# A relu-and-row-sum kernel whose first 8 MB block is loaded through two DMA queues instead of one

## The chip, the core and the metric

The kernel runs on one core of one Trainium2 chip. The core has five engines with their own instruction streams: TensorE (PE), VectorE (DVE), ScalarE (ACT), GpSimd (POOL) and SyncE (SP), and 16 DMA engines that move data between the chip's main memory (HBM) and the core's working memory (SBUF, 128 partitions). A DMA is issued by an instruction on one of the engines and goes into that engine's queue; when its data have landed it raises a semaphore on which other instructions wait. The metric is the device time of one execution in microseconds (us); lower is better. Before the change it is 161.0 us, the median of three runs (161.0, 161.0 and 161.11).

## The reference

```python
batch, seq, dim = 32, 512, 1024
x = randn(batch, seq, dim)          # float32, 64 MiB
relu_x = np.maximum(x, 0)
return np.sum(relu_x, axis=-1)      # (32, 512), float32
```

Each of the 16384 rows of 1024 numbers is clamped at zero from below and added up. The kernel reads 67.1 MB and writes 64 KB; there is nothing else to compute.

## The kernel before

**Tiling.** The 16384 rows are cut so that every partition of SBUF gets 128 rows: 16 rows from the first 2048 (`xf`), and 112 from the other 14336 (`xv`). In both parts the rows of one partition lie one behind the other in HBM. Seven blocks of 16 rows per partition (`ROWS = 16`, 8 MB each, 64 KB in one piece for each partition) are followed by a tail of 8 rows (4 MB), 4 rows (2 MB), and a last stretch of 4 rows, which comes in four loads that get ever smaller (1151, 436.5, 259 and 201.5 KB). Three buffers (`io0` to `io2`, `NBUF = 3`) of 8 MB take the blocks in turn.

**Who does what.** In blocks 0 and 1 ScalarE clamps the whole block in place with one instruction (`clamp`, line 145), and VectorE then adds up its 16 rows with one reduction (`total`, line 153). In blocks 2 to 4 the same is done in two halves of 8 rows, in block 5 in two pieces of 7 rows with two more rows left to ScalarE alone, which clamps and sums a row with one instruction (`act_row`, line 160). In block 6 and the tail ScalarE and VectorE each take whole rows (`act_row` and `dve_row`, line 168). The last stretch is divided among ScalarE, VectorE and GpSimd. TensorE does a few matmuls near the end whose results are not used.

**What sets the order.** All loads are issued by SyncE (`load`, line 104), so they stand in one queue in program order. The loads of blocks 0, 1 and 2 have a buffer each and wait for nothing. The load of block 3 waits on VectorE's semaphore until VectorE has finished block 0, whose buffer it overwrites; blocks 4, 5, 6 and the first tail load wait in the same way for blocks 1, 2, 3 and 4. Each load has a semaphore of its own (`sems.loads[n]`), which the DMA raises by 16 when it is complete.

**How it starts.** `open_without_barrier` takes the barriers of the program's opening out and moves SyncE's first load (`EARLY = 1`) in front of SyncE's first instruction, so the load of block 0 is the first thing that SyncE does. ScalarE's first instruction of this kernel's work is the load of its function table (`preload_act_table`, line 143). It waits for the semaphore of block 0's load (16), and stands for the wait of the first clamp too. The partial sums are collected in `res` and stored by three DMAs, two after the tail loads have been issued and one at the very end (line 116).

Of the kernel before, what the change touches and what calls it, by code (L numbers as in the profile page):

```python
# [5 lines left out]
RELU = mybir.ActivationFunctionType.Relu  # L6
# [3 lines left out]
ROWS = 16  # L10
NBUF = 3
# [14 lines left out]
MIDDLE_ACT, END_ACT = 214, 321  # L26

EARLY = 1
N_MM, MM_COLS = 8, 512


def kernel(tc: tile.TileContext, x: bass.AP, out: bass.AP):
    nc = tc.nc
    sems = Semaphores(tc)

    tc.close()
    tc.compile()
    nc.cur_bb = nc.bb_map[tc.start_bb_name]
    body = nc.cur_bb.bb.instructions
    ends = list(body)  # L40
    body.clear()
    n_stores = relu_sum(nc, sems, x, out)
    body.extend(ends)


    nc.cur_bb = nc.bb_map[tc.start_bb_name + "_end"]
    nc.cur_bb.bb.instructions.clear()
    nums = sorted(s.num for s in (*sems.loads, sems.act, sems.dve))
    cleared = range(nums[0], nums[-1] + 1)
    assert len(cleared) == len(nums)  # L50
    nc.sync.sem_clear(cleared)
    nc.sync.wait_ge(sems.stored, 16 * n_stores).then_inc(sems.stored, -16 * n_stores)
    open_without_barrier(tc, EARLY)

# [11 lines left out]
def relu_sum(nc, sems: Semaphores, x: bass.AP, out: bass.AP):  # L66
# [23 lines left out]
    def rows(m, n):  # L90
        if m < ROWS:
            return xf[:, m : m + n, :]
        return xv[:, m - ROWS : m - ROWS + n, :]

    def sums(m, n):
        if m < ROWS:
            return of[:, m : m + n], res[:, m : m + n]
        return ov[:, m - ROWS : m - ROWS + n], res[:, m : m + n]

    n_load = n_act = n_dve = n_store = 0  # L100

    def load(dst, src, after=None):
        nonlocal n_load
        dma = nc.sync.dma_start(out=dst, in_=src)  # L104
        if after:
            dma.wait_op(sems.dve, after[1], "sem-ge")
        dma.then_inc(sems.loads[n_load], 16)
        n_load += 1
        return sems.loads[n_load - 1]

    def store(m, n, act, sem, count):
        nonlocal n_store
        dst, src = sums(m, n)
        if act:
            nc.sync.wait_ge(sems.act, act)
        nc.sync.dma_start(out=dst, in_=src).wait_op(sem, count, "sem-ge").then_inc(
            sems.stored, 16
        )
        n_store += 1
# [20 lines left out]
    def clamp(ap, loaded):  # L140
        nonlocal n_act
        if n_act == 0:
            nc.scalar.preload_act_table(RELU).wait_op(loaded, 16, "sem-ge")  # L143
            loaded = None
        i = nc.scalar.activation(out=ap, in_=ap, func=RELU)  # L145
        if loaded is not None:
            i.wait_op(loaded, 16, "sem-ge")
        i.then_inc(sems.act, 1)
        n_act += 1

    def total(ap, m, n):
        nonlocal n_dve
        nc.vector.tensor_reduce(  # L153
            out=res[:, m : m + n], in_=ap, axis=mybir.AxisListType.X, op=ADD
        ).wait_op(sems.act, n_act, "sem-ge").then_inc(sems.dve, 1)
        n_dve += 1

    def act_row(ap, accum_out, loaded):
        nonlocal n_act
        i = nc.scalar.activation(out=ap, in_=ap, func=RELU, accum_out=accum_out)  # L160
        if loaded is not None:
            i.wait_op(loaded, 16, "sem-ge")
        i.then_inc(sems.act, 1)
        n_act += 1

    def dve_row(ap, accum_out, loaded):
        nonlocal n_dve
        i = nc.vector.tensor_scalar(  # L168
            out=ap,
            in0=ap,  # L170
            scalar1=0.0,
            scalar2=None,
            op0=MAX,
            op1=ADD,
            accum_out=accum_out,
        )
        if loaded is not None:
            i.wait_op(loaded, 16, "sem-ge")
        i.then_inc(sems.dve, 1)
        n_dve += 1  # L180
# [11 lines left out]
    freed = []  # L192
    m = 0
    for j in range(NB):
        buf = bufs[j % NBUF]
        loaded = load(buf[:, :, :], rows(m, ROWS), j >= NBUF and freed[j - NBUF])
        c = 0
        act_waits = dve_waits = loaded
        for n in TWO[j]:
            clamp(buf[:, c : c + n, :], act_waits)  # L200
            total(buf[:, c : c + n, :], m + c, n)
            act_waits = None
            c += n
        for _ in range(ACT[j]):
            act_row(buf[:, c, :], res[:, m + c : m + c + 1], act_waits)
            act_waits = None
            c += 1
        for _ in range(DVE[j]):
            dve_row(buf[:, c, :], res[:, m + c : m + c + 1], dve_waits)
            dve_waits = None  # L210
            c += 1
        assert c == ROWS
        freed.append((n_act, n_dve))
        m += ROWS
# [3 lines left out]
    buf = bufs[NB % NBUF]  # L218
    c = 0
    for n in TAIL:  # L220
        loaded = load(
            buf[:, c : c + n, :], rows(m, n), None if c else freed[NB - NBUF]
        )
# [9 lines left out]
    src = rows(m, 4).rearrange("p c d -> p (c d)")  # L233
    at = c * D
# [5 lines left out]
    loaded = load(flat[:, at : at + head], src[:, :head])  # L240
# [6 lines left out]
        out=clamped, in0=clamped, scalar1=0.0, scalar2=None, op0=MAX  # L247
    ).wait_op(loaded, 16, "sem-ge").then_inc(sems.end, 1)
    for lo, hi, n, first, second in (
# [3 lines left out]
        loaded = load(flat[:, at + lo : at + hi], src[:, lo:hi])  # L253
        act_part(flat[:, at + lo : at + lo + n], last[:, first : first + 1], (loaded, 16))
        dve_part(flat[:, at + lo + n : at + hi], last[:, second : second + 1], (loaded, 16))
    loaded = load(last[:, 2 : 2 + n_last], src[:, middle:end])
    assert loaded is sems.end

    store(0, ROWS, freed[0][0], sems.dve, freed[0][1])
    store(ROWS, NT - ROWS - 2, sums_act, sems.dve, sums_dve)


    all_there = (sems.end, 16 + 6)
    nc.vector.scalar_tensor_tensor(  # L266
        out=clamped,
# [6 lines left out]
    ).wait_op(*all_there, "sem-ge").then_inc(sems.end, 1)  # L274
    act_part(last[:, 2 + LAST_DVE :], res[:, NT - 1 : NT], all_there)
    store(NT - 2, 2, 0, sems.end, 16 + 6 + 2)
    return n_store


def open_without_barrier(tc: tile.TileContext, n_loads: int):  # L280

    SP = mybir.EngineType.SP
    blocks = tc.nc.main_func.blocks
    opening = blocks[0].instructions
    body = next(b for b in blocks if b.name == tc.start_bb_name).instructions
    for i in list(opening):
        if isinstance(i, (mybir.InstDrain, mybir.InstEventSemaphore)):
            opening.remove(i)  # L290
    loads = [i for i in body if i.engine == SP][:n_loads]
    for i in loads:
        assert isinstance(i, mybir.InstDMACopy)
        body.remove(i)
    at = next(n for n, i in enumerate(opening) if i.engine == SP)
    opening[at:at] = loads


# [28 lines left out]
```

## Time and profile before

| | |
|---|---|
| time, median of 3 runs | 161.0 us (161.0 to 161.11) |
| span of the profiled execution (first to last instruction) | 159.9 us |
| time of the runs that lies outside such a span | 161.0 - 159.9 = 1.1 us |
| time that the DMA queue's packets took, as a share of 16 engines' span | 97.8% |
| VectorE busy | 118.7 us (74%) |
| ScalarE busy | 103.6 us (65%) |
| HBM read | 67.11 MB, 420 GB/s over the span |

The page gives one execution, with the span from the first instruction to the last; the profiled execution has no other time of its own on the page. Busy shares are averages over the whole span. "Idle before" is the time in which an engine stood still ahead of a group of instructions, with what ended it. In the view by windows, the span is cut at given times; each row has the busy time of each engine with the number of its instructions in brackets, the granted TensorE clock, the share of the 16 DMA engines and GB/s. A DMA packet is booked in that view, with all its bytes and all its time, in the window in which it begins. In a short window the share can so be far over 1, and the GB/s say how many packets began there: a packet of block 0 is one partition's 64 KB (65,536 bytes).

### The profile page before, as it was taken

How to read it: one execution, taken by the hardware profiler on the slowest of the kernel's cores; microseconds unless marked ns; L12 is line 12 of the kernel's file. 1: busy time of each engine (PE TensorE's matmuls, PEld its weight loads, DVE VectorE, ACT ScalarE, POOL GpSimd, SP SyncE). 2: the span in 40 equal slices, each digit the busy share in tenths (PEclk: the TensorE clock that was granted, in tenths of full speed). 3: DMA queues.
4: the chain of work that ended last, by engine and by line, in shares of the span. 5: the costliest groups of instructions: out<-in, count | busy, mean ns of one | idle time of the engine just before them, and what ended most of it. 6: DMA issues, size and time to landing. Idle time of an engine off the chain costs nothing.

```text
span 159.9 us, 157 instructions
## 1 busy us (share of the span) xinstructions
PE 8.6 (5%) x16; PEld 3.6 (2%) x16; DVE 118.7 (74%) x44; ACT 103.6 (65%) x53; POOL 1.0 (1%) x5
## 2 busy tenths in 40 slices
PE   0000000000000000000000000000000000000695
PEld 0000000000000000000000000000000000000241
DVE  0000000006999799999999999999999799999986
ACT  0000049993599807997099950999429993397995
POOL 0000000000000000000000000000000000000001
DMA  8996996996996997999979979969969969899993
GB/s 279 508 492 295 524 492 295 524 492 295 525 492 295 524 475 311 524 393 393 525 328 459 508 344 459 508 295 508 492 295 524 492 295 524 377 402 402 428 396 110
DMA packets 2304, 67.18 MB, mean 420 GB/s; under 512 B 640, under 2 KB 768, under 8 KB 1024
## 3 DMA queue, kind: packets, MB, share of 16 engines
q1 hardware_dynamic: 2304, 67.18, 97.8%
HBM read 67.11 MB, written 0.07 MB: 420 GB/s over the span
## 4 chain that ended last, share of the span: by engine, by line
DMA 45%; DVE 45%; ACT 9%; SPq 1%; issue 0%
DMA io<-in_x_dram 45%; DVE res L153 43%; ACT io L145 9%; DVE io L168 1%; SPq L104 1%; DVE io L127 1%; DVE io L266 0%
## 5 line engine op out<-in xcount | busy, mean ns | idle before, releaser
L153 DVE TENSOR_REDUCE res<-io 128x8 f32<-128x8192 f32 (+2 forms) x10 | 101.1, 10173 | 39.2 <-ACT io L145 39.2
L145 ACT ACTIVATE io<-io 128x8192 f32<-128x8192 f32 (+2 forms) x10 | 81.8, 8218 | 25.9 <-DMA io<-in_x_dram 25.9
L160 ACT ACTIVATE io<-io 128x1024 f32<-128x1024 f32 x18 | 18.8, 1042 | 6.6 <-DMA io<-in_x_dram 6.6
L186 PE MATMUL ps<-io 128*128 128x512 f32 x16 | 8.6, 698 | 149.5 <-DVE io L168 149.5
L168 DVE TENSOR_SCALAR_CACHE_REDUCE io<-io 128x1024 f32<-128x1024 f32 x14 | 16.2, 1215 | 0.5 <-DMA io<-in_x_dram 0.4
L143 ACT ACT_TABLE_LOAD x1 | 1.3, 1283 | 22.3 <-DMA io<-in_x_dram 22.3
L186 PEld LDWEIGHTS ps<-io 128*128 128x128 f32 x16 | 3.6, 231 | 153.7 <-DVE io L168 149.5
L160 ACT ACTIVATION_READ_ACCUMULATOR io<-io 128x1 f32 x18 | 3.3, 186 | 0.0
L246 POOL TENSOR_SCALAR io<-io 128x254 f32<-128x254 f32 x1 | 0.8, 841 | 155.4 <-DMA io<-in_x_dram 155.4
L168 DVE DVE_READ_ACCUMULATOR io<-io 128x1 f32 x14 | 1.2, 82 | 0.0
L127 DVE TENSOR_SCALAR_CACHE_REDUCE io<-io 128x552 f32<-128x552 f32 (+1 forms) x2 | 1.1, 594 | 0.0
L122 ACT ACTIVATE io<-io 128x321 f32<-128x321 f32 (+1 forms) x2 | 0.9, 426 | 0.1
L266 DVE SCALAR_TENSOR_TENSOR io<-last,io 128x254 f32<-128x254 f32 x1 | 0.4, 423 | 0.0
L122 ACT ACTIVATION_READ_ACCUMULATOR io<-io 128x1 f32 x2 | 0.4, 186 | 0.0
L122 ACT ACTIVATE last<-last 128x153 f32<-128x153 f32 x1 | 0.3, 330 | 0.0
L122 ACT ACTIVATION_READ_ACCUMULATOR last<-last 128x1 f32 x1 | 0.2, 187 | 0.0
L127 DVE DVE_READ_ACCUMULATOR io<-io 128x1 f32 x2 | 0.2, 82 | 0.0
L311 POOL MEMSET const-uint8-127<- 128x1 uint8 x1 | 0.1, 102 | 0.0
L311 POOL MEMSET const-bfloat16-1.0<- 128x1 bf16 x1 | 0.1, 101 | 0.0
L311 POOL MEMSET const-float32-0.0<- 128x1 f32 x1 | 0.1, 99 | 0.2 <-issue 0.2
L311 POOL MEMSET const-float32-1.0<- 128x1 f32 x1 | 0.1, 98 | 0.0
L266 DVE DVE_READ_ACCUMULATOR io<-last,io 128x1 f32 x1 | 0.1, 82 | 0.0
## 6 DMA issues: line engine op xcount, KB each, us to landing
io<-in_x_dram SPq DMA_DIRECT2D x1, 4096.0 KB, 23.7
io<-in_x_dram SPq DMA_DIRECT2D x1, 2048.0 KB, 28.3
io<-in_x_dram SPq DMA_DIRECT2D x1, 1151.0 KB, 30.6
io<-in_x_dram SPq DMA_DIRECT2D x1, 436.5 KB, 31.2
io<-in_x_dram SPq DMA_DIRECT2D x1, 259.0 KB, 31.4
last<-in_x_dram SPq DMA_DIRECT2D x1, 201.5 KB, 31.4
io<-in_x_dram SPq DMA_DIRECT2D x7, 29.0
out_dram<-res SPq DMA_DIRECT2D x1, 55.0 KB, 1.6
```

Source lines behind the costliest of these rows:

```text
L104: dma = nc.sync.dma_start(out=dst, in_=src)
L122: nc.scalar.activation(out=ap, in_=ap, func=RELU, accum_out=accum_out).wait_op(*after, "sem-ge").then_inc(sems.end, 1)
L127: i = nc.vector.tensor_scalar(out=ap, in0=ap, scalar1=0.0, scalar2=None, op0=MAX, op1=ADD, accum_out=accum_out,)
L143: nc.scalar.preload_act_table(RELU).wait_op(loaded, 16, "sem-ge")
L145: i = nc.scalar.activation(out=ap, in_=ap, func=RELU)
L153: nc.vector.tensor_reduce(out=res[:, m : m + n], in_=ap, axis=mybir.AxisListType.X, op=ADD).wait_op(sems.act, n_act, "sem-ge").then_inc(se ...
L160: i = nc.scalar.activation(out=ap, in_=ap, func=RELU, accum_out=accum_out)
L168: i = nc.vector.tensor_scalar(out=ap, in0=ap, scalar1=0.0, scalar2=None, op0=MAX, op1=ADD, accum_out=accum_out,)
L186: i = nc.tensor.matmul(ps[:, :], rows_of[:, 0, :P], rows_of[:, 1, :MM_COLS], start=True, stop=True)
L246: nc.gpsimd.tensor_scalar(out=clamped, in0=clamped, scalar1=0.0, scalar2=None, op0=MAX).wait_op(loaded, 16, "sem-ge").then_inc(sems.end, 1)
L266: nc.vector.scalar_tensor_tensor(out=clamped, in0=last[:, : 2 + LAST_DVE], scalar=0.0, in1=clamped, op0=MAX, op1=ADD, accum_out=res[:, NT ...
L311: nc = _bacc.Bacc("TRN2", target_bir_lowering=False, num_devices=1)
```

## The change

The load of block 0 is split in two by partitions. The even partitions (64 of them, 4 MB) are loaded by a DMA from SyncE's queue, the odd ones (64, 4 MB) by a DMA from ScalarE's. Both raise the same semaphore by 16, and the first wait on it (the function table's on ScalarE) is for 32 instead of 16. `open_without_barrier` now moves the first load of SyncE and the first of ScalarE in front of the first instruction of their engines. All other loads, the stores and the computation are as they were.

```diff
 EARLY = 1
+QUEUES = 2
...
+    def load_spread(dst, src):
+        nonlocal n_load
+        for q, engine in enumerate((nc.sync, nc.scalar)):
+            engine.dma_start(out=dst[q::QUEUES], in_=src[q::QUEUES]).then_inc(
+                sems.loads[n_load], 16
+            )
+        n_load += 1
+        return sems.loads[n_load - 1]
...
     def clamp(ap, loaded):
         nonlocal n_act
         if n_act == 0:
-            nc.scalar.preload_act_table(RELU).wait_op(loaded, 16, "sem-ge")
+            nc.scalar.preload_act_table(RELU).wait_op(loaded, 16 * QUEUES, "sem-ge")
             loaded = None
...
     for j in range(NB):
         buf = bufs[j % NBUF]
-        loaded = load(buf[:, :, :], rows(m, ROWS), j >= NBUF and freed[j - NBUF])
+        first = j == 0
+        if first:
+            loaded = load_spread(buf[:, :, :], rows(m, ROWS))
+        else:
+            loaded = load(buf[:, :, :], rows(m, ROWS), j >= NBUF and freed[j - NBUF])
...
-    SP = mybir.EngineType.SP
...
-    loads = [i for i in body if i.engine == SP][:n_loads]
-    for i in loads:
-        assert isinstance(i, mybir.InstDMACopy)
-        body.remove(i)
-    at = next(n for n, i in enumerate(opening) if i.engine == SP)
-    opening[at:at] = loads
+    for engine in (mybir.EngineType.SP, mybir.EngineType.Activation):
+        loads = [i for i in body if i.engine == engine][:n_loads]
+        for i in loads:
+            assert isinstance(i, mybir.InstDMACopy)
+            body.remove(i)
+        at = next(n for n, i in enumerate(opening) if i.engine == engine)
+        opening[at:at] = loads
```

## The prediction

> **What bounds the kernel now.** I read the page's DMA line and queue share first:
>
> ```profile
> DMA  8996996996996997999979979969969969899993
> q1 hardware_dynamic: 2304, 67.18, 97.8%
> ```
>
> The 16 DMA engines are occupied for 97.8% of the span; the dips are an effect of booking a packet where it begins. Next the timeline between 37 and 125 us:
>
> ```profile
> 37.45 17.22 DVE L153 TENSOR_REDUCE res<-io 128x16 f32<-128x16384 f32 x1 [37.45 <-ACT io L145]
> 41.60 13.86 ACT L145 ACTIVATE io<-io 128x16384 f32<-128x16384 f32 x1 [4.18 <-DMA io<-in_x_dram]
> 54.70 70.41 SPq L104 DMA_DIRECT2D io<-in_x_dram  x6
> 60.95 13.95 ACT L145 ACTIVATE io<-io 128x8192 f32<-128x8192 f32 x2 [5.49 <-DMA io<-in_x_dram]
> 80.29 13.95 ACT L145 ACTIVATE io<-io 128x8192 f32<-128x8192 f32 x2 [5.39 <-DMA io<-in_x_dram]
> 99.65 13.95 ACT L145 ACTIVATE io<-io 128x8192 f32<-128x8192 f32 x2 [5.41 <-DMA io<-in_x_dram]
> ```
>
> The clamps start when a block lands, and blocks land every 19.35 us (60.95 - 41.60, 80.29 - 60.95). An 8 MB block is 128 packets of 64 KB, 8 for each of the 16 engines, so a packet takes 19.35 / 8 = 2.42 us, which is 27.1 GB/s per engine and 434 GB/s in all. ScalarE waits some 5.4 us for each block: compute is not the bound. The load of block 3 is issued at 54.70, while the block before it lands at 60.95, so the queue holds over 6 us of work. The chain of waits names VectorE for 43%, but only as the one that freed a buffer in time; the tail load that it released at 124.29 took 23.7 us to land by the table of DMA issues, though its own 8 packets per engine of half the size need 8 x 1.21 = 9.7 us: it stood in a queue that had not run dry. The end is thus: start of the DMA engines + 64 packets' worth of bytes on the slowest of them + the last arithmetic.
>
> Last the start, in windows:
>
> ```profile
> 0.00:1.00 1.00, 0.00 (x0) 0.00 (x0) 0.00 (x0) 0.00 (x0) 0.19 (x4) 1.00 0.00 0
> 1.00:1.50 0.50, 0.00 (x0) 0.00 (x0) 0.00 (x0) 0.00 (x0) 0.00 (x0) 1.00 4.62 1573
> 1.50:2.00 0.50, 0.00 (x0) 0.00 (x0) 0.00 (x0) 0.00 (x0) 0.00 (x0) 1.00 1.52 524
> 3.90:4.20 0.30, 0.00 (x0) 0.00 (x0) 0.00 (x0) 0.00 (x0) 0.00 (x0) 1.00 2.02 874
> 4.20:4.60 0.40, 0.00 (x0) 0.00 (x0) 0.00 (x0) 0.00 (x0) 0.00 (x0) 1.00 3.78 1638
> 4.60:4.80 0.20, 0.00 (x0) 0.00 (x0) 0.00 (x0) 0.00 (x0) 0.00 (x0) 1.00 0.00 0
> 4.80:5.00 0.20, 0.00 (x0) 0.00 (x0) 0.00 (x0) 0.00 (x0) 0.00 (x0) 1.00 1.51 655
> ```
>
> GB/s times window over 65,536 bytes gives the packets that begin: 12 between 1.0 and 1.5 us, 4 between 1.5 and 2.0. A first packet takes 4.62 x 0.5 x 16 / 12 = 3.08 us, 0.66 more than a later one. Second packets begin on 14 engines between 3.9 and 4.6, and on the last two between 4.8 and 5.0. These two stay behind for good, since all do the same work at the same pace, and a load is complete only with them.
>
> **The change part by part.** The sum is made against the profiled 159.9 us, and 161.0 - 159.9 = 1.1 us outside the span is carried over to compare with the median.
>
> *One more DMA on ScalarE.* SyncE's load issues take 0.33 to 0.49 us (0.41 median). ScalarE's next work, the table load, waits until 22.27 us, so the issue costs nothing there; uncovered it would be 0.5 us.
>
> *When the odd half starts.* No row shows when ScalarE begins; GpSimd's first row is at 0.23 us, so I take some 0.2 us after SyncE. An engine has an even packet to move until 3.9 us at the earliest, so an odd packet that is ready by 2 us or so costs nothing. The bounds are -0.4 (ScalarE's half lets engines begin one issue earlier) and +0.7; I take 0.
>
> *SyncE's queue.* The loads of blocks 1 and 2 stand behind a DMA of half the size and are issued no later. The wait for 32 ends with the later half. If the DMA engines take the two queues' packets in turn, the eight packets of block 0 on each engine still go first, and block 0 lands where it did.
>
> *How 64 rows fall to 16 engines.* This decides. The whole load gives each engine 8 of 128 partitions; each half gives it 4 of 64, and the trace doesn't say which. In all stages the pace is 2.42 us per packet on every engine, but with the whole load an engine and its group of partitions are one to one, so the rows can't tell an engine's limit from a limit of the way into a group of 8 partitions. If the limit is the engine's, or the halves are dealt to the same groups, the cost is 0. If the limit is the group's, and the 64 rows are dealt in another pattern, two engines write into one group at a time while another group gets nothing. Each then has half of the 27.1 GB/s, and the 8 packets of block 0 take 8 x 4.84 instead of 8 x 2.42 us: +19.35 us. From this goes what the offsets between engines give back: an engine that is d ahead of its partner leaves the shared group d earlier, and takes the next one alone for d, so 2d; with first packets that begin over 1.0 to 2.0 us, d is about 0.3, and 0.6 comes off: +18.75. The nearest row (the 8 MB load of block 1) lacks just this point, since it is one DMA over all partitions. I take the far end, at even odds, because the one constant ceiling in every stage, whatever the source addresses, looks more like a fixed way into SBUF than like reads that vary (first packets vary, later ones don't), and because a half load's rows have to fall exactly as before to keep the groups apart.
>
> [...]
>
> No stage hides the 18.75 us. Block 0 would land at 22.3 + 18.75 = 41.0, block 1 at 41.6 + 18.75 = 60.3, and every later landing, clamp, buffer release and load issue moves by the same amount, so the 6 us in the queue stay as they are. Sum: 159.9 + 18.75 + 0 + 0 = 178.7, with 1.1 outside 179.8 us. Own range: 178.1 (d of 0.9, so 17.55, and 0.45 from the first rival) to 181.1 (no d, and the late start's 0.7).
>
> **The rivals.**
>
> *The start gets more even (faster).* If a half load reaches all engines sooner, or the second queue's packet fills the 0.66 us of a first packet's delay, the two late engines catch up. They lag 4.8 to 5.0 against 4.2 to 4.6 for most, so 0.45 us, and 161.0 - 0.45 = 160.5 us (to 160.3, if all begin like the first). For it: the late engines set every landing. Against it: nothing in the rows ties the stagger to the length of the load. It counts as faster from 0.32 us on, that is if the two late engines gain at least that and no group is shared.
>
> *Nothing happens (same).* The half loads keep the groups and the pace and the start stays as it is: 161.0, 160.7 to 161.3. [...]
>
> *Changing queues costs time per packet.* No row has two queues in turn. From below it is the same queue's 0; from above the first packet's 0.66, for 8 packets 5.3 us. Near the lower end, 0.15 each, it is 1.2 us: 162.2 (161.4 to 166.3). From 0.04 us a packet on it is measurable.
>
> *SyncE's queue is served first.* Then block 1 goes ahead of the odd half, and block 0 is whole only at about 41.6. Table load 1.3, clamp 13.9 and reduction 17.2 end at 74.0 instead of 54.7; the load of block 3 is issued then, its packets begin 1.0 later with a first packet's 0.66, and the engines have been dry since about 60.9: 75.0 + 0.7 - 60.9 = 14.8 us, 175.8 us. Against it: the odd half's packets are ready before the first even packet ends.
>
> **How the numbers follow.** Shared groups 0.50, more even start 0.26, nothing 0.09, price per packet 0.10, SyncE first 0.05. About 0.2% (0.32 us) is what a measurement of this kernel can tell from no change. Faster 0.26, same 0.09, slower 0.50 + 0.10 + 0.05 = 0.65. The predicted time is the likeliest case's, 179.8. The range has to reach into the faster case to leave out no more than 0.2: 160.5 to 181.1 leaves out half of that case, 0.13, and little above; inside it, the stretch between 167 and 175 is nearly empty.
>
> **What would show it.** Right: block 0's packets take about 4.8 us each, the function table loads at about 41 us, and block 1 lands 19.35 us after that at the old 2.42 a packet. If packets of block 0 take 2.42 us and the table loads at about 22 us, the groups aren't shared and the forecast is wrong by its main term; the windows of the second packets then show whether the two late engines caught up, and gaps between packets show a price per change. A table load at 22 us with a later end would be something not thought of here.

## The result and the profile after

The changed kernel takes 161.55 us, the median of 12 runs (161.35 to 161.65), against 161.03 us for 12 runs of the kernel before. The ratio is 1.0027 with a 95% interval of 1.0019 to 1.0035: slower by 0.4 to 0.5 us, a small loss clear of noise. Neither the forecast of 179.8 us nor the gain of the first rival came.

The page of the changed kernel shows the second queue (packets, MB, share of 16 engines):

```profile
q1 hardware_dynamic: 2240, 62.98, 91.8%
q10 hardware_dynamic: 80, 4.19, 6.1%
```

ScalarE's queue is q10, with 80 packets: 64 of 64 KB, 4.19 MB, and 16 of 4 bytes. The two shares add to the 97.8% of before within 0.1. The timeline of the changed kernel from the start:

```profile
0.00 0.55 SPq L115 DMA_DIRECT2D io<-in_x_dram  x1
0.12 0.55 ACTq L115 DMA_DIRECT2D io<-in_x_dram  x1
0.60 54.45 SPq L105 DMA_DIRECT2D io<-in_x_dram  x3
22.30 1.28 ACT L153 ACT_TABLE_LOAD   x1 [22.30 <-DMA io<-in_x_dram]
41.52 13.86 ACT L155 ACTIVATE io<-io 128x16384 f32<-128x16384 f32 x1 [4.07 <-DMA io<-in_x_dram]
60.86 7.03 ACT L155 ACTIVATE io<-io 128x8192 f32<-128x8192 f32 x1 [5.49 <-DMA io<-in_x_dram]
```

ScalarE issues its half 0.12 us after SyncE. The table load comes at 22.30 us, and in the profile before at nearly the same time:

```profile
22.27 1.28 ACT L143 ACT_TABLE_LOAD   x1 [22.27 <-DMA io<-in_x_dram]
```

Block 1 lands at 41.5 us (41.6 before). In this pair of profiles nothing is late; below it turns out that the profile before is not a typical one. What differs is the length of an issue: 0.55 us for a half load, where the whole load's took 0.38 us. The windows of the changed kernel, with the packets booked where they begin:

```profile
1.00:1.50 0.50, 0.00 (x0) 0.00 (x0) 0.00 (x0) 0.00 (x0) 0.00 (x0) 1.00 2.70 918
1.50:2.00 0.50, 0.00 (x0) 0.00 (x0) 0.00 (x0) 0.00 (x0) 0.00 (x0) 1.00 2.91 1049
2.00:2.50 0.50, 0.00 (x0) 0.00 (x0) 0.00 (x0) 0.00 (x0) 0.00 (x0) 1.00 0.32 131
4.20:4.60 0.40, 0.00 (x0) 0.00 (x0) 0.00 (x0) 0.00 (x0) 0.00 (x0) 1.00 3.78 1638
4.60:5.00 0.40, 0.00 (x0) 0.00 (x0) 0.00 (x0) 0.00 (x0) 0.00 (x0) 1.00 2.27 983
6.60:7.00 0.40, 0.00 (x0) 0.00 (x0) 0.00 (x0) 0.00 (x0) 0.00 (x0) 1.00 3.40 1475
```

By 1.5 us only 7 first packets have begun (12 before), 8 follow until 2.0 and one after it; in the trace's packet records the first begins at 1.34 us instead of 1.01. The second packets begin on 10 engines between 4.2 and 4.6 and on 6 between 4.6 and 5.0: there is no pair left behind, but the field as a whole is later. By the packet records the first 128 packets begin in eight sets of 16, the first set SyncE's, the second ScalarE's, the third SyncE's and so on: the queues take strict turns, packet by packet. Such a packet takes 3.40 x 0.4 x 16 / 9 = 2.42 us, exactly as before.

In the chain of waits of the changed kernel the end has the same links as before, each some 0.1 us earlier in this one execution (before: 55.49, 125.15 and 155.75):

```profile
55.40 68.79 DVE res L163 x7
125.06 30.57 DMA io<-in_x_dram
155.65 1.23 DVE io L178 x2
```

So the two profiled executions both have a span of 159.9 us, and the loss is not to be seen in them. For that one has to look at all runs, each of which lists its time and its span. In the runs of the experiments, the kernel before has spans of 159.66 us on average (20 runs beside the first experiments; 159.5 to 159.8), and 1.33 us outside the span. The profiled 159.9 us was a long one, and the 1.1 us that the table of before and the prediction put outside the span were too few. The profiles of the experiments show where it was long. In ten of them block 0 is loaded as before, whole and from SyncE. Their table loads come at 21.76 to 22.00 us, 21.89 on average, and by their packet records no engine begins its second packet after 4.74 us. One of the ten (`g4_four_more_act`):

```profile
21.93 1.28 ACT L143 ACT_TABLE_LOAD   x1 [21.93 <-DMA io<-in_x_dram]
```

The two engines that began their second packets between 4.8 and 5.0 us belong to that one execution, then, and not to the kernel. The five profiles that begin with two loads of every second partition (the changed kernel's and four of the experiments') have their table loads at 22.12 to 22.43 us, 22.30 on average. Beside the ten, block 0 is some 0.4 us late.

The changed kernel's 12 runs have a span of 159.94 us and 1.56 us outside. The loss has two parts: some 0.3 us inside the span and 0.23 us outside it.

### The profile page after: what moved, and what is told of

Same layout as the page of the kernel before. It is cut to its first block, busy times and chain, and to the rows that moved or that the text cites. A ratio compares the mean times of both kernels' runs of the same rounds, so it can differ in the third digit from the quotient of the medians.

```text
span 159.9 us, 158 instructions
## 1 busy us (share of the span) xinstructions
PE 8.6 (5%) x16; PEld 3.6 (2%) x16; DVE 118.8 (74%) x44; ACT 103.6 (65%) x53; POOL 1.0 (1%) x5
## 3 DMA queue, kind: packets, MB, share of 16 engines
q10 hardware_dynamic: 80, 4.19, 6.1%
## 4 chain that ended last, share of the span: by engine, by line
DVE 45%; DMA 45%; ACT 9%; SPq 1%; issue 0%
DMA io<-in_x_dram 45%; DVE res L163 43%; ACT io L155 9%; DVE io L178 1%; DVE io L137 1%; SPq L105 0%; SPq L115 0%; DVE io L280 0%
```

## The experiments

Three theories for the two parts stood at first: that a second queue in the program costs (outside the span), that two issues at the same moment disturb each other (inside), and that a load of half the partitions is dearer to start (inside). Times are medians, spans means of the runs, "outside" the median of each run's time less its span (the runs list spans to 0.1 us); "before" is always the kernel before on the same chip.

**Both halves from SyncE's queue** (`e1_both_on_sp`)

```diff
-        for q, engine in enumerate((nc.sync, nc.scalar)):
+        for q, engine in enumerate((nc.sync, nc.sync)):
...
-    for engine in (mybir.EngineType.SP, mybir.EngineType.Activation):
-        loads = [i for i in body if i.engine == engine][:n_loads]
+    for engine in (mybir.EngineType.SP,):
+        loads = [i for i in body if i.engine == engine][: 2 * n_loads]
```

> Even and odd half both from SyncE's queue, as its first two instructions; ScalarE issues no DMA. Three theories for the 0.5 us that the changed kernel takes longer while its profiled span is no longer than before (159.9 us; 1.6 us lie outside it instead of 1.1). Second queue: using ScalarE's queue at all costs about 0.5 us outside the span; then this kernel is at 161.0 us, with 1.1 outside. Two issues at once: issues on two engines at the same moment slow each other (0.55 us instead of 0.38) and put the first packets off to 1.3 us; then the first issue here is back at 0.4 us, packets begin at about 1.0, and the time is 161.0 or a little over. The form: a load of every second partition is itself dearer to issue; then the issue here takes 0.55 us too and the time is 161.4 to 161.6.

Measured: 161.41 us (ratio 1.0026, 1.0016 to 1.0036), span 160.04 against 159.66, outside 1.38. Its timeline and its windows:

```profile
0.00 1.18 SPq L115 DMA_DIRECT2D io<-in_x_dram  x2
```

```profile
1.00:1.50 0.50, 0.00 (x0) 0.00 (x0) 0.00 (x0) 0.00 (x0) 0.00 (x0) 1.00 2.79 918
1.50:2.00 0.50, 0.00 (x0) 0.00 (x0) 0.00 (x0) 0.00 (x0) 0.00 (x0) 1.00 2.64 918
2.00:2.50 0.50, 0.00 (x0) 0.00 (x0) 0.00 (x0) 0.00 (x0) 0.00 (x0) 1.00 0.65 262
```

Two issues in 1.18 us, so 0.55 to 0.58 each though nothing is issued beside them, and again 7 packets by 1.5 us. Two issues at once are not the cause; the form of the load is left. It costs 0.38 us in the span. The part outside is nearly gone, as the second queue would have it.

**ScalarE's half left in its place** (`e2_act_after_opening`)

```diff
-    for engine in (mybir.EngineType.SP, mybir.EngineType.Activation):
+    for engine in (mybir.EngineType.SP,):
```

> The changed kernel, but ScalarE's half is not moved in front of its opening: it is issued where ScalarE enters the body. Second queue: 161.5 us, 1.6 outside the span, as in the changed kernel. Two issues at once: ScalarE's issue comes later, so SyncE's first issue is nearer to 0.4 us, its packets begin at about 1.0 to 1.1, and the time falls to 161.0 to 161.2.

Measured: 161.53 us (1.0039, 1.0026 to 1.0051), outside 1.53. ScalarE's issue began at 0.12 us all the same, so this says nothing on two issues at once: the move to the front of ScalarE's program is worth nothing here.

**One store on ScalarE's queue, the start as before** (`e3_store_from_act`; edit of the kernel before, at the end of the loop over blocks)

```diff
+        if j == 2:
+            dst, src = sums(0, ROWS)
+            nc.scalar.dma_start(out=dst, in_=src).wait_op(
+                sems.dve, freed[0][1], "sem-ge"
+            ).then_inc(sems.stored, 16)
+            n_store += 1
...
-    store(0, ROWS, freed[0][0], sems.dve, freed[0][1])
```

> The kernel before with one thing changed: the 8 KB store of the sums of block 0 is issued by ScalarE, after its clamps of block 2, instead of by SyncE near the end. The start is that of before. Second queue: about 161.5 us, with the span at 159.9 and 1.6 outside. Two issues at once, or the form: 161.0, 1.1 outside.

Measured: 161.23 us (1.0014, 1.0006 to 1.0023), span 159.65 against 159.66, outside 1.58. It looked as if the second queue were the cause of the part outside. That fell later.

**Block 0 whole on ScalarE's queue** (`e4_whole_on_act`)

```diff
-        for q, engine in enumerate((nc.sync, nc.scalar)):
-            engine.dma_start(out=dst[q::QUEUES], in_=src[q::QUEUES]).then_inc(
-                sems.loads[n_load], 16
-            )
+        nc.scalar.dma_start(out=dst, in_=src).then_inc(sems.loads[n_load], 16)
...
-            nc.scalar.preload_act_table(RELU).wait_op(loaded, 16 * QUEUES, "sem-ge")
+            nc.scalar.preload_act_table(RELU).wait_op(loaded, 16, "sem-ge")
```

> Block 0 whole, 128 partitions in one load, as ScalarE's first instruction; SyncE begins with the load of block 1. Not split, but two queues. Second queue: 1.6 outside the span. Two issues at once: both issues 0.5 us or more and first packets at 1.3 us, as in the changed kernel. The packets of blocks 0 and 1 take turns, so block 0 lands at about 41 us instead of 22.3; the buffer of block 0 is then released at about 74 us, the queue runs dry after block 2, and by the working of my last rival the time is about 175 us (170 to 177), with 13 us more in the span.

Measured: 178.38 us (1.1078, 1.1063 to 1.1093), outside 1.74 (four runs, 1.56 to 1.85). Its timeline:

```profile
0.12 0.39 ACTq L114 DMA_DIRECT2D io<-in_x_dram  x1
41.25 1.28 ACT L150 ACT_TABLE_LOAD   x1 [41.25 <-DMA io<-in_x_dram]
73.68 17.45 SPq L105 DMA_DIRECT2D io<-in_x_dram  x2
```

With 128 partitions the issue is back at 0.39 us beside SyncE's own, which settles the point on two issues at once. Block 0 lands at 41.25, as it would if its packets and block 1's take turns, and the load of block 3 is issued at 73.68, where my last rival had 74.0. The loss is 17.4 us instead of the 14.8 that I had priced. Part of the other 2.6 us lies outside the span (0.4 us more than before), and part at the end, which is no longer set by the loads. By the chain of waits, VectorE works from 56.43 us on without waiting for a load, and the matmuls whose results are not used come last:

```profile
56.43 100.96 DVE res L160 x10
166.55 9.64 PE ps L193 x16
```

**Contiguous halves** (`e5_partition_halves`), the test of the forecast's own assumption

```diff
-            engine.dma_start(out=dst[q::QUEUES], in_=src[q::QUEUES]).then_inc(
+            engine.dma_start(out=dst[q * 64 : q * 64 + 64], in_=src[q * 64 : q * 64 + 64]).then_inc(
```

> The changed kernel with partitions 0 to 63 from SyncE's queue and 64 to 127 from ScalarE's, instead of even and odd. If the 27.1 GB/s are the limit of the way into a group of partitions (the assumption under my forecast), 16 engines press into half of the groups in each half load: packets of block 0 of about 4.8 us, the table load at about 41 us, 178 to 180 us. If the limit is the engine's, nothing changes against the changed kernel: packets of 2.42 us, 161.5 us. On the issue: if 64 rows are dear, the issue is 0.55 us and the first packets begin at 1.3 us; if the step over partitions is, 0.38 us and 1.0 us.

Measured: 181.43 us (1.1268, 1.1253 to 1.1284), outside 1.60; a little more than the 178 to 180 us of the first case. Its timeline, and its windows:

```profile
0.00 0.55 SPq L115 DMA_DIRECT2D io<-in_x_dram  x1
42.39 1.28 ACT L153 ACT_TABLE_LOAD   x1 [42.39 <-DMA io<-in_x_dram]
61.47 13.86 ACT L155 ACTIVATE io<-io 128x16384 f32<-128x16384 f32 x1 [3.93 <-DMA io<-in_x_dram]
```

```profile
1.00:1.50 0.50, 0.00 (x0) 0.00 (x0) 0.00 (x0) 0.00 (x0) 0.00 (x0) 1.00 5.58 1180
6.00:7.00 1.00, 0.00 (x0) 0.00 (x0) 0.00 (x0) 0.00 (x0) 0.00 (x0) 1.00 4.99 1049
```

Between 6 and 7 us 16 packets begin (1049 x 1.0 over 65.5 KB), one on each engine, and a packet takes 4.99 x 16 / 16 = 4.99 us, about twice the 2.42. The table loads at 42.39 us. Here is the picture that I had forecast, in another cut. The first packets are as slow (5.58 x 0.5 x 16 / 9 = 4.96 us). The packet records show why the second queue is no help: the first 16 packets are SyncE's, the next 16 ScalarE's, the next 16 SyncE's again, so all 16 engines are in the same half of the partitions nearly all the time. All of them are occupied, and the block still moves at half the pace, so the limit is not the engines' own. Even and odd partitions, with the same number of rows and packets, do not run into it (2.42 us a packet). Where the limit lies is not shown: the two half loads differ from the even and odd ones in taking 64 neighbouring partitions and in reading one stretch of 4 MB each in HBM, and no run parts the two. The issue is 0.55 us again, so for a first load it goes with the number of partitions and not with the step over them.

**Halves by rows, two queues** (`e6_row_halves`) **and one queue** (`e7_row_halves_on_sp`; with the edits of the first experiment besides)

```diff
-            engine.dma_start(out=dst[q::QUEUES], in_=src[q::QUEUES]).then_inc(
+            engine.dma_start(out=dst[:, q * 8 : q * 8 + 8], in_=src[:, q * 8 : q * 8 + 8]).then_inc(
```

> The changed kernel split by rows: rows 0 to 7 of every partition from SyncE's queue, rows 8 to 15 from ScalarE's. Two queues, but each load has all 128 partitions. If the loads over every second partition cost the 0.3 us at the start, the issue is back at 0.38 us, the first packets begin at 1.0 us, and only the 0.23 us outside the span stay: 161.2 us. If it is the split in itself, 161.5.

> The same split by rows, both loads from SyncE's queue. With neither a second queue nor half the partitions both costs should be gone: 161.0 us, issue 0.38 us, first packets at 1.0 us, 1.33 us outside the span. If the split in itself costs, 161.3 or more.

> The changed kernel itself, on the same chip as these three: 161.5 us, 0.3 us more in the span than the kernel before and 0.2 us more outside it.

Measured: 161.27 us with two queues (1.0018, 1.0009 to 1.0027), span 159.71, outside 1.57; 160.98 with one (0.9998, 0.9990 to 1.0007), span 159.65, outside 1.36; the changed kernel itself (`e8_changed_again`) 161.55, span 159.98, outside 1.57; before 161.01, 159.68 and 1.32. The timeline of the kernel with two queues, then that with one:

```profile
0.00 0.37 SPq L115 DMA_DIRECT2D io<-in_x_dram  x1
0.12 0.38 ACTq L115 DMA_DIRECT2D io<-in_x_dram  x1
```

```profile
0.00 0.85 SPq L115 DMA_DIRECT2D io<-in_x_dram  x2
```

And a window of the kernel with two queues, whose packets are of 32 KB:

```profile
1.00:1.50 0.50, 0.00 (x0) 0.00 (x0) 0.00 (x0) 0.00 (x0) 0.00 (x0) 1.00 2.55 721
```

With 128 partitions in each load the issues take 0.37 to 0.43 us, the first packets begin at 1.0 us (11 by 1.5 us: 721 x 0.5 over 32.8 KB), and the part inside the span is gone. A split in itself costs nothing.

**The split by partitions where the start is covered** (`e9_block1_even_odd`; the kernel before, with block 1 in two loads and its clamp waiting for 32)

```diff
+    def load_spread(dst, src):
+        nonlocal n_load
+        for q in range(2):
+            nc.sync.dma_start(out=dst[q::2], in_=src[q::2]).then_inc(sems.loads[n_load], 16)
...
+        if j == 1:
+            loaded = load_spread(buf[:, :, :], rows(m, ROWS))
```

> The kernel before, with the load of block 1 instead of block 0 split into even and odd partitions, both from SyncE's queue. If the 0.35 us that a split by partitions costs at the start come from the longer issue and the later first packets alone, they are hidden here, since block 0 keeps the DMA engines occupied until 22 us: issues of about 0.55 us for the two halves, 161.0 us. If half the partitions also cost something while the packets move, the span is longer here too: 161.3 us.

Measured: 161.01 us against 160.93 (1.0001, 0.9992 to 1.0010), span 159.65 against 159.62. Its timeline:

```profile
0.00 0.38 SPq L104 DMA_DIRECT2D io<-in_x_dram  x1
0.43 1.16 SPq L114 DMA_DIRECT2D io<-in_x_dram  x2
1.64 0.58 SPq L104 DMA_DIRECT2D io<-in_x_dram  x1
```

The halves of block 1 take 0.53 and 0.59 us to issue, and nobody waits for them. So the 0.3 us of the change are the start of the first load and nothing else. The last line is the whole load of block 2: right behind a half load it too takes 0.58 us to issue, where it took 0.43 us in the kernel before. So in these runs only the first load of an engine has an issue whose length goes with the number of partitions.

**Four stores on ScalarE's queue** (`e10_four_stores_act`)

```diff
+        if j == 2:
+            for k in range(4):
+                dst, src = sums(4 * k, 4)
+                i = nc.scalar.dma_start(out=dst, in_=src)
+                i.wait_op(sems.dve, freed[0][1], "sem-ge")
+                i.then_inc(sems.stored, 16)
...
-    store(0, ROWS, freed[0][0], sems.dve, freed[0][1])
```

> The store of the sums of block 0, which the earlier experiment moved to ScalarE's queue as one DMA, in four DMAs of 4 columns each on that queue. If the 0.24 us outside the span are a price for having the second queue in the program, they stay 0.24: 161.25 us with 1.55 to 1.6 outside. If each DMA on that queue costs, they are four times as much: 162.0 us with 2.3 outside.

Measured: 161.06 us (1.0008, 0.9999 to 1.0016), outside 1.35. Neither expectation: with four DMAs on the second queue the price is not four times as high, it is gone. Its table of DMA issues shows that they are there:

```profile
out_dram<-res ACTq DMA_DIRECT2D x4, 2.0 KB, 50.1
```

A price for having the second queue would have stayed. But this kernel ran on another chip than those with one DMA, so the chip was a suspect too, and the number of instructions on ScalarE a third. The next four ran on one chip.

**One, four and two stores; one ScalarE instruction more without a DMA** (`f1_one_store_act` and `f2_four_stores_act` are the two kernels above again; `f3_two_stores_act` has `range(2)` and 8 columns each; `f4_one_more_act` is the kernel before with)

```diff
-            clamp(buf[:, c : c + n, :], act_waits)
+            if j == 2 and c == 0:
+                clamp(buf[:, 0:4, :], act_waits)
+                clamp(buf[:, 4:8, :], None)
+            else:
+                clamp(buf[:, c : c + n, :], act_waits)
```

> One store on ScalarE's queue once more, now beside the four-store kernel. If what lies outside the span depends on the chip, it is near 1.35 us here on another chip, or 1.58 with the four-store kernel at 1.58 too. If one DMA on that queue costs and four don't, 1.58 here and 1.35 there: 161.2 and 161.0 us.

> Four stores on ScalarE's queue once more, on the same chip as one and two: 1.35 us outside if it is the number of instructions, the same as with one store if it is the chip.

> The same store in two DMAs on ScalarE's queue. A price that goes by the place of ScalarE's last instructions in its program, not by the queue, would be there or gone here in one step: 1.35 or 1.58 us outside, and nothing in between.

> The kernel before with one more instruction on ScalarE and no DMA there: the first clamp of block 2 is made in two pieces of 4 rows. Second queue: 1.33 us outside, 161.0 us. Number of ScalarE's instructions: 1.55 to 1.6 us outside, 161.2 us, as with one DMA more on that engine.

Measured, with 1.34 us outside for the kernel before: one store 161.21 us (1.0017, 1.0008 to 1.0026), outside 1.53; two stores 161.35 (1.0022, 1.0013 to 1.0031), outside 1.67; four stores 160.98 (1.0002, 0.9993 to 1.0011), outside 1.37; one clamp more 161.16 (1.0010, 1.0001 to 1.0019), outside 1.48. It is not the chip, since one store and four still differ on the same one, and a price for having the second queue is out. Two stores lie higher than one, so it isn't one step either. And one more instruction without any DMA costs 0.14 us outside the span, so the queue is not needed for it.

**Two, three and four more clamps; the changed kernel with three more** (`g2_two_more_act`, `g3_three_more_act`, `g4_four_more_act`, `g1_changed_three_more_act`: the first clamp of block 2 in 3, 4, 5 and 4 pieces; shown with 4)

```diff
+            if j == 2 and c == 0:
+                for lo, hi in ((0, 2), (2, 4), (4, 6), (6, 8)):
+                    clamp(buf[:, lo:hi, :], act_waits if lo == 0 else None)
```

> The changed kernel, with the first clamp of block 2 made in four pieces, so that ScalarE has four instructions more than before the change, as in the four-store kernel. If the part outside the span goes by the number of ScalarE's instructions, it falls from 1.57 to about 1.37 us, and only the start's 0.35 us stay: 161.35 us. If it is the second queue: 161.55, 1.57 outside.

> The kernel before with two more instructions on ScalarE (three clamps for one) and no DMA there. By the number of instructions: 1.67 us outside, as with two stores; 161.3 us. By the queue: 1.34, 161.0.

> Three more instructions on ScalarE, no DMA there. By the number of instructions, somewhere between the 1.67 us of two and the 1.37 us of four: 161.0 to 161.4 us. By the queue: 1.34, 161.0.

> Four more instructions on ScalarE, no DMA there. By the number of instructions: 1.37 us outside, 161.0 us. A price that only grows with each instruction would give 1.8 or more, 161.5 us.

| ScalarE instructions more than before | outside the span, store moved from SyncE in 1, 2 or 4 DMAs | outside the span, clamps added |
|---|---|---|
| 0 | 1.34 | 1.33 |
| 1 | 1.53 | 1.48 |
| 2 | 1.67 | 1.65 |
| 3 | | 1.48 |
| 4 | 1.37 | 1.34 |

The times go with it: 161.30 us for two clamps more (1.0020, 1.0011 to 1.0029), 161.05 for three (1.0007, 0.9998 to 1.0015), 161.00 for four (1.0003, 0.9994 to 1.0012). The changed kernel with three more clamps, and so four ScalarE instructions more than before, takes 161.31 us (1.0020, 1.0011 to 1.0029): span 159.95 against 159.64, outside 1.34 against 1.33. The 0.23 us outside are gone from the changed kernel while its two queues stay. So the number of ScalarE's instructions, and not the second queue, decides whether they are there; by what means isn't shown. What remains of the loss is the start:

```profile
0.00 0.54 SPq L115 DMA_DIRECT2D io<-in_x_dram  x1
0.12 0.55 ACTq L115 DMA_DIRECT2D io<-in_x_dram  x1
```

(The timeline of that kernel.) No version was faster than the kernel before beyond noise; the split by rows on one queue equals it.

## Why the prediction was wrong

*The bound, and what hides what: right.* The DMA engines set the time, at 2.42 us a packet from 4 us on; ScalarE's issue cost nothing on ScalarE; its half began 0.12 us after SyncE's, where I took 0.2; and a later start went through to the end undiminished: in the profiles block 0 lands 0.4 us later on average, and the spans are 0.4 us longer (160.05 for the five, 159.63 for the ten).

*How 64 rows fall to 16 engines: the step that failed.* I put +18.75 us for engines that share a group of partitions at even odds. One half of its reasoning stands: there is a ceiling other than the engine's own, as the contiguous halves show (4.99 us a packet where I had 4.84, a span 20.2 us longer), though no run shows that it lies in the way into the partitions, or that there are groups of 8 of them with a limit each; these were my assumption. The other half failed: I had assumed that 64 even or odd rows are dealt in a pattern that makes two engines share a group. Their packets take 2.42 us, as in the whole load, so no engine gets into another's way, and the term was 0. The nearest row, a load over all 128 partitions, would have given the right value. I went against it with an argument (rows would have to fall "exactly as before") for which no row stood. How the rows are dealt isn't visible in the trace; only that the even and odd halves don't collide is shown.

*The start of SyncE's half: missing from the sum.* I wrote that the loads behind it are issued "no later" and bounded only the odd half's start. That a first load of 64 partitions takes 0.17 us longer to issue, and that its first packets begin 0.33 us later, had no term. In the span it measured 0.30 us (changed kernel), 0.38 us (both on SyncE) and 0.31 us (with three more clamps). Why it is so stays open: that for a first load it goes with the number of partitions is shown, the reason is not.

*The 1.1 us outside the span, "carried over": wrong twice.* It was 1.33 us before, as the profiled execution was a long one, and it doesn't stay the same under an edit. It rose to 1.56 us with the one instruction more that the change gives ScalarE; one store more on ScalarE gave 1.53 and 1.58 us, one clamp more 1.48 us. With three clamps more in the changed kernel it was back at 1.34 us.

*The rivals.* The more even start had nothing to win: the two late engines, from which I had taken its 0.45 us, belong to the one execution that I had read, and the whole field began later. "Nothing happens" was right on the pace (2.42 us a packet), and missed the two small costs (0.30 us inside the span, 0.23 us outside it). The price per packet for changing queues is 0: packets in turn take 2.42 us. SyncE's queue is not served first; the queues take turns from the second packet on (16 packets of ScalarE's behind SyncE's first 16). SyncE gains no issue time over the kernel before, since its first issue grew from 0.38 to 0.55 us; with both halves on SyncE it is through with them at 1.18 us.

*Luck.* That the time rose, to which I had given 0.65, came true by two costs that I hadn't priced. And 161.55 us lies inside the range only because the range had been drawn down to 160.5 us for the first rival's sake.

## What to carry to other kernels

Here the DMA engines never ran dry (97.8% of the span), and a second queue had nothing to give. The first load was best in the form that started soonest: all 128 partitions, 0.38 us to issue against 0.55 for 64. If a load must be cut by partitions, try even and odd first (2.42 us a packet here) and not neighbouring halves (4.99 us a packet, half the pace). And below some 0.3 us, look at span and time outside it one by one, and add a few harmless instructions to the engine that was edited, before a difference is put down to what the edit does.

## What the runs showed of the hardware that was not expected

The time outside the span went with the number of ScalarE's instructions: 1.33, 1.48, 1.65, 1.48 and 1.34 us with 0, 1, 2, 3 and 4 more, up to 0.3 us, and back where it began with four. Where in the launch or the end it arises wasn't tried. One more instruction on SyncE moved it by 0.05 us at most (1.36 and 1.38 against 1.32 and 1.33). The kernel with block 0 whole on ScalarE's queue, with one instruction more there, doesn't fit in (1.74 us, four runs); why stays open.

As the first of their engine, loads of 64 partitions took 0.54 to 0.56 us to issue, alone or beside another, with and without a step over partitions, and loads of 128 partitions 0.37 to 0.39 us. Further back this doesn't hold: right behind a half load, a load of 128 partitions took 0.57 to 0.59 us, and as the fourth load in a row it took 0.55 us in the kernel with both row halves on SyncE; as the second or third behind whole loads it took 0.42 to 0.43 us. What sets it there stays open.
